# A two-block layer on one core: LRU steps dealt out over a whole period, and GpSimd's products on ScalarE and VectorE

## The chip, the core and the metric

One core of a Trainium2 chip runs the whole program. The metric is the device time of one execution in microseconds; each run of a kernel gives one time. Engines are named as the profile names them: PE is TensorE's matmul, PEld its weight load, DVE VectorE, ACT ScalarE, POOL GpSimd, SP SyncE, which issues most of the transfers.

## What is computed

Two layers follow each other on one sequence of 512 positions and 1024 channels, in float32. The first layer normalises the input, projects it, and merges three branches: a state-space scan (SSD), a gated linear recurrent unit (LRU) and attention to 256 memory rows. The second does the same with forgetting attention, an S5 state-space model and another memory attention. Cut to the parts that matter here:

```python
h = rms_norm(x, norm_g)
proj = h @ w_in                       # z, xbc, dt, lru_gate, lru_x, q, gate_logits
xl = causal_dwconv(lru_x, lru_conv_w, lru_conv_b)          # 4 taps
y_lru = rg_lru(xl, ...) * silu(lru_gate)
merged = g0 * (y_ssd @ w_br_ssd) + g1 * (y_lru @ w_br_lru) + g2 * (y_mem @ w_br_mem)

def rg_lru(x, w_a, b_a, w_x, b_x, lam):                    # 16 blocks of 96 channels
    r = sigmoid(x @ w_a + b_a); i = sigmoid(x @ w_x + b_x)
    log_a = -8 * r * softplus(-lam)
    a = exp(log_a); u = sqrt(-expm1(2 * log_a)) * (i * x)
    return scan(h[t] = a[t] * h[t-1] + u[t])
```

## The kernel before

Everything is kept with channels on the 128 partitions and the 512 positions along the free axis, so a tile is 128x512. A float32 product is made of three fast passes: each operand is split into a high part, rounded to TensorE's short format, and the rest, the low part; high x high, low x high and high x low are summed in PSUM. ScalarE makes the high part of a weight tile (`whi`, L267), VectorE the low part (`wlo`, L280).

The program is a list, `prog`, of jobs and steps. A job is one weight tile of up to 128x1024, in two halves; a half is 12 matmuls of 512 columns for a projection (6 or 9 for others). Before each half, `issue` (L237) puts in the loads two jobs ahead, the high part of the weights four halves ahead and the low part three ahead (`split`, `split_low`), then the steps that are due, then the half's matmuls, and after the second half its evacuation. All engines run their instructions in the order in which this writes them. A step is placed by hand: `lay` (L226) puts named steps in front of numbered halves (`x3@8` is step x3 ahead of half 8), and `after(n, f)` (L190) makes f due n halves later. TensorE has PSUM tiles of three kinds: `gtile` and `xtile`, two buffers each, and `stile`, four. A projection can begin only when the evacuation of the one before the last has read its buffer.

Four places matter here:

- **Input's norm** (`norm_steps`, L529, laid out at L716 among the halves of the memory's key and value projections, `kv_jobs`). Steps x0 to x7 load x, Q0 to Q7 square it and add (ScalarE and GpSimd), T0 and T1 make the reciprocal root (statistics, then rows), g0 to g7 multiply by it on GpSimd (L552), f0 to f7 split the result into high and low parts with the gain (L558 ScalarE, L559 VectorE).
- **Warm matmuls** (`warm`, L708): nine 128x128 products of ones at the start.
- **LRU groups** (L912): the 1536 channels go in four groups s = 0 to 3 of three tiles. A group's gates (`lru_gate`, with the small matmuls for blocks that cross tiles, whose operands `lru_edges` copies between partitions by DMA) take four short halves; then come the three `lru_sg` projections, whose silu is kept, between which `lru_a` (decay `la`, its square on GpSimd, L867, and two products), `lru_b` (square root on ScalarE, then product and scan, L879 and L880) and `lru_c` (product with the silu on GpSimd, L891, and the split of the result, `split_y`) are put in. Then come the projections of the next group (`lru_in`: convolution of four taps, L783 and three times L785, and a split) and the filler: the eight halves that project this group's result, summed into `acc`.
- **Second block's first projections** (L1766): k, v, q and gate of the first pair of heads. `fox_vt` (step v0, L1659) turns v by four transposes (L1663).

Of the kernel before, what the change touches and what calls it, by code (L numbers as in the profile page):

```python
# [171 lines left out]
def two_blocks(ctx, tc, A, out):  # L172
# [356 lines left out]
    def norm_steps(src, gain, dst, queue):  # L529
# [21 lines left out]
        def times(k):  # L551
            return lambda: G.tensor_tensor(st["x"][k], st["x"][k], st["r"], ALU.mult)  # L552

        def fin(k):
            def run():
                x = st["x"][k]
                hi, lo = hp_tile("hhi", k, F32R), hp_tile("hlo", k, F32R)
                S.activation(hi, x, AF.Copy, scale=gain(k))  # L558
                V.scalar_tensor_tensor(lo, x, gain(k), hi.bitcast(F32), ALU.mult, ALU.subtract)  # L559
                dst.append((hi, lo))  # L560
            return run
# [146 lines left out]
    def warm():  # L708

        ps = stile()  # L710
        for _ in range(9):
# [4 lines left out]
    lay(kvj, "c0@1 c1@1 c2@1 c3@1 s4@3 s5@2 s6@2 s7@2 x0@4 x1@4 t0@5 x2@6 t1@7 Q0@7 x3@8 Q1@8 x4@10 Q2@10 x5@12 Q3@12 x6@14 Q4@14 x7@15 Q5@16 "  # L716
        "Q6@18 Q7@19 T0@21 T1@22 g0@22 g1@23 g2@23 g3@23 f0@24 g4@24 f1@25 g5@25 f2@26 g6@26 "
        "f3@27 g7@27 f4@28 f5@29 f6@30 f7@31",
# [60 lines left out]
    add(closed("mlp"), opened("lrp"), g2b[3:])  # L779
# [77 lines left out]
    def lru_a(s):  # L857
        L = lru[s]

        def tile_(j):  # L860
# [6 lines left out]
            G.tensor_tensor(a2, a, a, ALU.mult)  # L867
# [3 lines left out]
        for j in range(3):  # L871
            after(j, (lambda j: lambda: tile_(j))(j))

    def lru_b(s):
        L = lru[s]

        def tile_(j):
# [3 lines left out]
        for j in range(3):  # L881
            S.activation(L["r"][0][j], L["r"][0][j], AF.Sqrt, scale=-1.0 / 16)
        for j in range(3):
            after((j if s == 3 else j + 1) if j < 2 or s < 3 else 2, (lambda j: lambda: tile_(j))(j))

    def lru_c(s):
        L = lru[s]

        def tile_(j):
# [3 lines left out]
        for j in range(3):  # L893
# [18 lines left out]
    for s in range(4):  # L912
        add(lru_gate(s, 0), lru_gate(s, 1))
        add(lru_sg(s, 0), lambda s=s: lru_a(s), lru_sg(s, 1), lambda s=s: lru_b(s), lru_sg(s, 2),
# [1069 lines left out]
```

## Time and profile before

| what | value |
|---|---|
| median of three runs | 1688.86 us (1682.77, 1688.86, 1692.17) |
| the profiled execution | 1688.69 us, its span 1687.0 us |
| PE busy | 1630.0 us, 97% |
| DVE busy | 1160.3 us, 69% |
| ACT busy | 784.7 us, 47% |
| POOL busy | 440.4 us, 26% |

The span is the time from the first to the last instruction that the profiler saw. All times in rows are microseconds from its start. A busy share is an average over all stages, so what a change in one stage is worth has to be read from that stage's own rows: who waits there, for whom, and what follows the wait. Matmuls overlap, so the busy time of PE is that of modelled intervals; how fast TensorE goes is better read from how many matmuls a piece of the chain of waits holds and how long that piece is.

### The profile page before, as it was taken

What the parts mean: (1) busy time and instruction counts of PE and PEld (TensorE: products, weight loads), DVE (VectorE), ACT (ScalarE), POOL (GpSimd) and SP (SyncE); (2) the same over time, 40 slices, a digit from 0 to 9 for tenths busy, and PEclk for the clock granted to TensorE, in tenths of its full rate; (3) what the DMA queues carried; (4) which work ended last, traced back from release to release, by engine and by line L of the source; (5) the groups of instructions that cost most, each with busy time, mean ns of one, the idle gap of its engine ahead of it and who ended that gap; (6) DMA issues with size and microseconds to landing.
All of it is one profiled execution on the core that took longest, in us unless ns stands there. A gap on an engine that the chain in (4) does not pass through costs nothing.

```text
span 1687.0 us, 23007 instructions
## 1 busy us (share of the span) xinstructions
PE 1630.0 (97%) x8202; PEld 1333.5 (79%) x8202; DVE 1160.3 (69%) x1871; ACT 784.7 (47%) x1532; POOL 440.4 (26%) x636
## 2 busy tenths in 40 slices
PE   9999999999999999999999999998999999999998
PEld 8788887787788787878787786777787888888886
DVE  7753267768645987687767886888887545775554
ACT  6554345654543545554544654334344333544334
POOL 4200001211201422213143493665656000020002
PEclk9999999999999999999999999999999999999999
DMA  7322233243323343333432555444334323232532
GB/s 246 120 66 87 85 115 94 90 130 100 95 89 121 106 124 122 97 120 109 133 109 97 177 159 183 109 121 107 102 97 106 122 86 105 94 103 91 174 101 87
DMA packets 112834, 193.01 MB, mean 114 GB/s; under 512 B 50576, under 2 KB 57892, under 8 KB 112720
## 3 DMA queue, kind: packets, MB, share of 16 engines
q1 hardware_dynamic: 97984, 181.41, 34.5%
q10 hardware_dynamic: 14736, 10.14, 2.2%
q8 instruction: 65, 1.06, 0.3%
q14 instruction: 49, 0.40, 0.1%
HBM read 173.90 MB, written 9.54 MB: 109 GB/s over the span
## 4 chain that ended last, share of the span: by engine, by line
PE 67%; DVE 20%; ACT 5%; issue 4%; DMA 3%; POOL 0%; SPq 0%; ACTq 0%; DVEq 0%; POOLq 0%
PE g L351 47%; PE x L351 6%; DVE wlo L280 4%; PE s L351 1%; PE s L1931 1%; DMA rstd<-rs_d 1%; DVE mx L1693 1%; ACT whi L267 1%; DVE P L1700 1%; PE x L1103 1%; PE x L1720 1%; DVE acc L1641 1%; DVE ys L1137 1%; PE x L1107 1%; DVE rg L879 1%
## 5 line engine op out<-in xcount | busy, mean ns | idle before, releaser
L351 PE MATMUL g<-hlo,whi 128*128 128x512 f32 x1304 | 515.9, 396 | 0.0
L280 DVE TENSOR_TENSOR wlo<-wraw,whi 128x512 fp32r<-128x512 f32 (+1 forms) x556 | 424.8, 778 | 102.9 <-ACT whi L267 91.4
L267 ACT ACTIVATE whi<-wraw 128x512 fp32r<-128x512 f32 (+1 forms) x556 | 331.1, 607 | 234.7 <-PE g L351 98.5
L351 PE MATMUL g<-hhi,whi 128*128 128x512 f32 x832 | 331.7, 399 | 10.5 <-DVE xl L785 8.2
L351 PEld LDWEIGHTS g<-hlo,whi 128*128 128x128 f32 x1304 | 249.1, 191 | 51.0 <-issue 1.0
L351 PE MATMUL g<-hhi,wlo 128*128 128x512 f32 x832 | 224.4, 392 | 0.0
L351 PE MATMUL g<-mrg,whi 128*128 128x512 f32 x536 | 219.6, 410 | 0.0
L351 PEld LDWEIGHTS g<-hhi,whi 128*128 128x128 f32 x832 | 157.3, 189 | 47.5 <-issue 11.4
L351 PEld LDWEIGHTS g<-hhi,wlo 128*128 128x128 f32 x832 | 157.6, 189 | 33.6
L351 PE MATMUL g<-mrg,wlo 128*128 128x512 f32 x536 | 144.4, 391 | 0.0
L351 PEld LDWEIGHTS g<-mrg,whi 128*128 128x128 f32 x536 | 103.5, 193 | 22.9 <-issue 1.9
L351 PEld LDWEIGHTS g<-mrg,wlo 128*128 128x128 f32 x536 | 101.6, 190 | 22.2
L351 PE MATMUL g<-y,whi 128*128 128x512 f32 x432 | 114.2, 399 | 5.0 <-DVE t L785 2.3
L867 POOL TENSOR_TENSOR t<-la 128x512 f32<-128x512 f32 x12 | 18.2, 1514 | 321.6 <-ACT la L864 321.6
L351 PEld LDWEIGHTS g<-y,whi 128*128 128x128 f32 x432 | 79.9, 188 | 27.4 <-issue 2.7
L351 PE MATMUL x<-y,whi 128*128 128x512 f32 x336 | 85.3, 393 | 0.5 <-ACT whi L267 0.5
L785 DVE SCALAR_TENSOR_TENSOR t<-g,p,t 128x511 f32<-128x511 f32 (+2 forms) x72 | 53.9, 748 | 38.3 <-ACT t L783 36.6
L1080 POOL TENSOR_SCALAR_AFFINE_SELECT M<-M 128x512 f32<-128x512 f32 x32 | 25.5, 802 | 200.7 <-DMA M<-acs_d 94.7
L351 PEld LDWEIGHTS x<-y,whi 128*128 128x128 f32 x336 | 62.8, 188 | 14.9 <-ACT whi L267 1.3
L1859 POOL TENSOR_TENSOR hhi<-hhi,t 128x512 f32<-128x512 f32 x8 | 13.0, 1626 | 222.1 <-DVE t L1858 210.6
L351 PE MATMUL g<-y,wlo 128*128 128x512 f32 x216 | 61.4, 393 | 0.0
L1694 ACT ACTIVATE P<-P,mx 128x128 f32<-128x128 f32 (+3 forms) x48 | 27.0, 563 | 69.1 <-DVE mx L1693 66.0
(593 smaller groups left out, 2798.7 us busy)
## 6 DMA issues: line engine op xcount, KB each, us to landing
wraw<-in_w_in SPq DMA_DIRECT2D x164, 512.0 KB, 3.3
M<-acs_d SPq DMA_DIRECT2D x32, 256.0 KB, 4.5
wraw<-in_w_ssd SPq DMA_DIRECT2D x16, 512.0 KB, 3.4
wraw<-in_w_out SPq DMA_DIRECT2D x16, 512.0 KB, 3.5
wraw<-in_w_v SPq DMA_DIRECT2D x12, 512.0 KB, 3.7
wraw<-in_w_mem SPq DMA_DIRECT2D x12, 512.0 KB, 3.3
wraw<-in_w_lru SPq DMA_DIRECT2D x16, 384.0 KB, 3.0
wraw<-in_w_k SPq DMA_DIRECT2D x11, 512.0 KB, 4.8
```

The costliest lines, as they stand in the source:

```text
L267: S.activation(hi, raw, AF.Copy)
L280: V.tensor_tensor(lo, raw, hi.bitcast(F32), ALU.subtract)
L351: PE.matmul(ps, w, X[k0 + k][low], start=(k0 + p == 0), stop=(k0 + n == nk and p == 3 * n - 1))
L785: V.scalar_tensor_tensor(dst[:, sft:], ps[:, :512 - sft], c1(cwn, (3 - sft) * nt + j), dst[:, sft:], ALU.mult, ALU.add)
L867: G.tensor_tensor(a2, a, a, ALU.mult)
L879: V.tensor_tensor(u, u, L["r"][0][j], ALU.mult)
L1080: G.affine_select(M, M, [[0, 4], [1, 128]], ALU.is_ge, NEG, base=0, channel_multiplier=-1)
L1103: PE.matmul(py[64 * q_:64 * q_ + 64, c * 128:c * 128 + 128], R["xdt"][:, c, (2 * j + q_) * 64:(2 * j + q_) * 64 + 64], M[:, c])
L1107: PE.matmul(po[:, c * 128:c * 128 + 128], R["prev"][c][:, j * 128:j * 128 + 128], R["C"][:, c * 128:c * 128 + 128])
L1137: V.scalar_tensor_tensor(y, y, c1("ssd_ng", 4 * g + i), R["rs"], ALU.mult, ALU.mult)
L1641: V.tensor_tensor(kl[a][hf], t[hf], k[a][hf].bitcast(F32), ALU.subtract)
L1694: S.activation(P[:, :n], P[:, :n], AF.Exp, bias=mx[:, 0:1], accum_out=mx[:, 1:2])
```

## The change

- In the LRU groups the steps are one function, `lru_steps`, called after the first silu projection; it deals the steps out over the halves that follow: gates at 0, 2 and 4, the three roots at 5, product and scan at 6, 8 and 10, the product with the silu at 12, 14 and 16. The split of the result goes into the next group's gate halves (`lru_parts` at 1, 2 and 3). In the last group, which has no next one, the products come at 8, 9 and 11.
- So a group's result is projected one group later: the filler of group s is the projection of group s - 1. Group 0 has no earlier result; its filler is two gate projections and the second half of the memory branch, which stood ahead of the groups before. Between the first `lru_in` projections and the first gates stand three gate projections, six halves, instead of the memory branch's eight.
- The square of the decay is a Square on ScalarE and the product with the silu a product on VectorE, 12 of each; both were on GpSimd.
- In the input's norm, VectorE multiplies x by gain and reciprocal root in one operation (`scalar_tensor_tensor`), eight times, in place of GpSimd; the split is then a plain one. The steps are laid out anew: loads and squares sooner, statistics three halves sooner, products and splits from half 20 to 31.
- Twelve warm matmuls instead of nine.
- v0 stands ahead of half 7 of the second block's first projections instead of half 5.

```diff
         def times(k):
-            return lambda: G.tensor_tensor(st["x"][k], st["x"][k], st["r"], ALU.mult)
+            return lambda: V.scalar_tensor_tensor(st["x"][k], st["x"][k], gain(k), st["r"], ALU.mult, ALU.mult)
         def fin(k):
             def run():
-                x = st["x"][k]
                 hi, lo = hp_tile("hhi", k, F32R), hp_tile("hlo", k, F32R)
-                S.activation(hi, x, AF.Copy, scale=gain(k))
-                V.scalar_tensor_tensor(lo, x, gain(k), hi.bitcast(F32), ALU.mult, ALU.subtract)
+                split_to(hi, lo, st["x"][k])
...
-        for _ in range(9):
+        for _ in range(12):
...
-    lay(kvj, "c0@1 c1@1 c2@1 c3@1 s4@3 s5@2 s6@2 s7@2 x0@4 x1@4 t0@5 x2@6 t1@7 Q0@7 x3@8 Q1@8 x4@10 Q2@10 x5@12 Q3@12 x6@14 Q4@14 x7@15 Q5@16 "
...
+    lay(kvj, "c0@1 c1@1 c2@1 c3@1 s4@3 s5@2 s6@2 s7@2 x0@4 x1@4 t0@5 x2@6 t1@7 x3@7 Q0@7 x4@8 Q1@8 Q2@9 x5@10 Q3@10 x6@11 x7@12 Q4@12 "
...
-    add(closed("mlp"), opened("lrp"), g2b[3:])
+    add(closed("mlp"), opened("lrp"))
...
-            G.tensor_tensor(a2, a, a, ALU.mult)
+            S.activation(a2, a, AF.Square)
...
+        def times(j):
             u = L["r"][1][j]
-            G.tensor_tensor(u, u, L["sg"][j], ALU.mult)
-            L["Y"].append(split_y(u))
-        for j in range(3):
-            after(0 if s == 3 else j + 1, (lambda j: lambda: tile_(j))(j))
+            V.tensor_tensor(u, u, L["sg"][j], ALU.mult)
+
+        staged(gates, 0, 2, 4)
+        staged(roots, 5)
+        staged(scan, 6, 8, 10)
+        staged(times, *((8, 9, 11) if s == 3 else (12, 14, 16)))
+        if s == 3:
+            staged(lambda j: lru_parts(3, j), 11)
+
+    def lru_parts(s, j):
+        lru[s]["Y"].append(split_y(lru[s]["r"][1][j]))
 
     add([lru_in(0, j) for j in range(3)])
-    add(branch_jobs(A["w_mem"], 4, Late(Ym, 4), 4, mem_last, xtile))
+    add(g2b[3:6])
...
     for s in range(4):
...
+        if s:
+            add((lambda s: lambda: staged(lambda j: lru_parts(s - 1, j), 1, 2, 3))(s))
+        add(lru_gate(s, 0), lru_gate(s, 1), lru_sg(s, 0), lambda s=s: lru_steps(s), lru_sg(s, 1), lru_sg(s, 2))
         if s < 3:
-            br = branch_jobs(A["w_lru"], 4 * s, Late(lru[s]["Y"], 0), 3, acc_first() if s == 0 else acc_add, xtile)
-            add([lru_in(s + 1, j) for j in range(3)], br)
+            add([lru_in(s + 1, j) for j in range(3)])
+        add(fill if s else [g2b[6:], branch_jobs(A["w_mem"], 4, Late(Ym, 4), 4, mem_last, xtile)])
+        fill = branch_jobs(A["w_lru"], 4 * s, Late(lru[s]["Y"], 0), 3, acc_first() if s == 0 else acc_add, xtile)
+    add(lambda: [lru_parts(3, j) for j in (1, 2)])
...
-    lay(fi, "u0@2 n0@5 v0@5 n1@6",
+    lay(fi, "u0@2 n0@5 n1@6 v0@7",
```

`staged(f, *at)` makes f(j) due at[j] halves later. What the change moves on VectorE is seen at three places. The first is group 2, from the last silu projection to the first tile of the next group. L455 ends a silu, L879 and L880 are product and scan of one tile, L388 is the low half of a result, L785 the convolution. VectorE's order before:

```order
L455 SCALAR_TENSOR_TENSOR sg<-t,g 128x512
L280 TENSOR_TENSOR wlo<-wraw,whi 128x512
L879 TENSOR_TENSOR rg_3333<-rg_3333,rg_3299 128x512
L880 SCALAR_TENSOR_TENSOR rg_3333<-la,rg_3333 128x512
L388 TENSOR_TENSOR y<-rg_3313,y 128x512
L280 TENSOR_TENSOR wlo<-wraw,whi 128x512
L388 TENSOR_TENSOR y<-rg_3325,y 128x512
L785 SCALAR_TENSOR_TENSOR xl<-g,p_92,xl 128x511
```

And now, where the same lines are L455, L880, L881, L388 and L783, with L870 and L871 for the two products of a gate:

```order
L870 SCALAR_TENSOR_TENSOR rg_3208<-rg_3208,xl 128x512
L871 SCALAR_TENSOR_TENSOR rg_3170<-t,rg_3170 128x512
L455 SCALAR_TENSOR_TENSOR sg<-t,g 128x512
L280 TENSOR_TENSOR wlo<-wraw,whi 128x512 x2
L880 TENSOR_TENSOR rg_3188<-rg_3188,rg_3146 128x512
L881 SCALAR_TENSOR_TENSOR rg_3188<-la,rg_3188 128x512
L783 SCALAR_TENSOR_TENSOR xl<-g,p_92,xl 128x511
```

Ahead of the convolution of the first next tile stands one scan, that of tile 0, and no low half of a result; the other two scans have moved behind it.

The second place is the end of group 3. Before, VectorE's last steps stood with the last silu (L455) ahead of the split of the next small job's weights (L276):

```order
L879 TENSOR_TENSOR rg_3834<-rg_3834,rg_3800 128x512
L880 SCALAR_TENSOR_TENSOR rg_3834<-la,rg_3834 128x512
L455 SCALAR_TENSOR_TENSOR sg<-t,g 128x512
L388 TENSOR_TENSOR y<-rg_3814,y 128x512
L388 TENSOR_TENSOR y<-rg_3826,y 128x512
L388 TENSOR_TENSOR y<-rg_3834,y 128x512
L276 TENSOR_TENSOR whi<-wraw,whi 128x4x32
```

Now the sums of the filler (L675) stand among the products with the silu (L885) and the scans:

```order
L880 TENSOR_TENSOR rg_3701<-rg_3701,rg_3663 128x512
L881 SCALAR_TENSOR_TENSOR rg_3701<-la,rg_3701 128x512
L885 TENSOR_TENSOR rg_3689<-rg_3689,sg 128x512
L675 TENSOR_TENSOR acc<-acc,x 128x512
L280 TENSOR_TENSOR wlo<-wraw,whi 128x384
L885 TENSOR_TENSOR rg_3701<-rg_3701,sg 128x512
```

The last silu has gone ahead of all of these, and each sum has a step of the group before or behind it.

The third place is the input's norm, VectorE again. Before, from the end of the first value projection (VVl), a split of x (L559) stood between two low halves of weights, and its product was GpSimd's:

```order
L393 TENSOR_TENSOR KTl<-t,KT 128x256
L601 SCALAR_TENSOR_TENSOR VVl<-g,mrc,VV 128x512 x2
L559 SCALAR_TENSOR_TENSOR hlo<-acc,p_92,hhi 128x512
L280 TENSOR_TENSOR wlo<-wraw,whi 128x512
```

Now each of its steps is a split (L393) and a product (L552), and they begin ahead of the end of that projection:

```order
L393 TENSOR_TENSOR hlo<-acc,hhi 128x512
L552 SCALAR_TENSOR_TENSOR acc<-acc,p_92,rstd 128x512
L280 TENSOR_TENSOR wlo<-wraw,whi 128x512
L393 TENSOR_TENSOR KTl<-t,KT 128x256
L599 SCALAR_TENSOR_TENSOR VVl<-g,mrc,VV 128x512 x2
```

VectorE has two operations per tile of x where it had one, and three tiles have been begun when that projection ends.

## Rows read from the trace of the kernel before

**Rows 1.** The page: busy time, share of the span, instructions of each engine.

```profile
PE 1630.0 (97%) x8202; PEld 1333.5 (79%) x8202; DVE 1160.3 (69%) x1871; ACT 784.7 (47%) x1532; POOL 440.4 (26%) x636
```

**Rows 2.** Waits of PE: who waited for whom, us in total, times, longest.

```profile
PE g L351 <- DVE xl L785: 8.2, 3, 2.7
PE x L597 <- DVE wlo L280: 3.1, 3, 1.7
...
PE s L1663 <- DVE t L1325: 2.8, 1, 2.8
...
PE g L938 <- DVE sg L455: 2.2, 1, 2.2
...
PE g L351 <- ACT whi L267: 1.1, 1, 1.1
```

**Rows 3.** The chain that ended last: start us, length us, what, number.

```profile
244.31 5.50 PE g L351 x24
...
274.40 7.32 PE g L351 x24
...
451.93 5.53 PE g L938 x16
...
1035.49 9.79 PE g L351 x36
```

**Rows 4.** Stretches: length, busy us of each engine (instructions), granted clock, DMA share, GB/s.

```profile
10.00:15.00 5.00, 5.00 (x25) 4.98 (x24) 4.23 (x9) 3.42 (x8) 1.80 (x3) 0.50 0.60 224
274.40:277.80 3.40, 3.40 (x9) 2.63 (x10) 3.37 (x6) 1.66 (x3) 0.00 (x0) 0.53 0.37 116
```

**Rows 5.** DVE in time, group 0: start, length, line, operation, names, shapes, number.

```profile
253.91 1.53 DVE L868 SCALAR_TENSOR_TENSOR rg<-rg,xl 128x512 f32<-128x512 f32 x1
...
259.21 0.68 DVE L280 TENSOR_TENSOR wlo<-wraw,whi 128x512 fp32r<-128x512 f32 x1
259.82 0.68 DVE L879 TENSOR_TENSOR rg<-rg,rg 128x512 f32<-128x512 f32 x1
260.53 1.23 DVE L880 TENSOR_TENSOR_SCAN rg<-la,rg 128x512 f32<-128x512 f32 x1
...
262.25 1.79 DVE L879 TENSOR_TENSOR rg<-rg,rg 128x512 f32<-128x512 f32 x1
...
271.95 2.30 DVE L785 SCALAR_TENSOR_TENSOR xl<-g,p,xl 128x511 f32<-128x511 f32 x3
```

**Rows 6.** POOL in time, group 0.

```profile
253.36 1.53 POOL L867 TENSOR_TENSOR t<-la 128x512 f32<-128x512 f32 x1 [0.70 <-ACT la L864]
...
261.90 1.59 POOL L891 TENSOR_TENSOR rg<-rg,sg 128x512 f32<-128x512 f32 x1 [4.96 <-DVE rg L880]
```

**Rows 7.** ACT by line, 0 to 70 us: busy us, mean ns, idle before.

```profile
L424 ACT ACTIVATE t<-acc 128x512 f32<-128x512 f32 x8 | 5.0, 620 | 0.3 <-DMA acc<-in_xT 0.3
```

**Rows 8.** ACT in time, group 0: the load of the square root's table.

```profile
256.65 1.28 ACT L882 ACT_TABLE_LOAD   x1
```

**Rows 9.** The copies into the edge tiles xe, from issue to landing.

```profile
DMA to landing us min/median/max: 2.6/3.9/5.5
```

**Rows 10.** DVE in time, the input's norm.

```profile
50.99 1.73 DVE L559 SCALAR_TENSOR_TENSOR hlo<-acc,p,hhi 128x512 fp32r<-128x512 f32 x1
...
57.70 1.79 DVE L559 SCALAR_TENSOR_TENSOR hlo<-acc,p,hhi 128x512 fp32r<-128x512 f32 x1
```

**Rows 11.** POOL in time, the input's norm.

```profile
46.45 12.49 POOL L552 TENSOR_TENSOR acc<-acc,rstd 128x512 f32<-128x512 f32 x8 [5.07 <-ACT rstd L419]
```

**Rows 12.** DVE in time, second block's first projections.

```profile
1034.13 0.65 DVE L1325 SCALAR_TENSOR_TENSOR t<-g,r 128x512 f32<-128x512 f32 x1
...
1039.88 0.69 DVE L1323 TENSOR_TENSOR t<-g,r 128x512 f32<-128x512 f32 x1 [3.05 <-PE g L351]
```

**Rows 13.** POOL in time, the same place.

```profile
1040.30 1.68 POOL L1674 TENSOR_SCALAR_AFFINE_SELECT nbm<-nb 128x512 f32<-128x512 f32 x2 [15.93 <-DMA nb<-n_d]
```

**Rows 14.** PE in time, the first scores.

```profile
1045.13 0.28 PE L1686 MATMUL s<-hhi 128*128 128x256 f32 x1
```

More of the change, by code (lines that the diff above doesn't have):

```diff
@@ L715, in two_blocks @@
     named = {"c": msc[4:], "t": mstat, "Q": xsq, "s": msq, "T": xstat, "f": xfin, "g": xrow, "x": xload}
-    lay(kvj, "c0@1 c1@1 c2@1 c3@1 s4@3 s5@2 s6@2 s7@2 x0@4 x1@4 t0@5 x2@6 t1@7 Q0@7 x3@8 Q1@8 x4@10 Q2@10 x5@12 Q3@12 x6@14 Q4@14 x7@15 Q5@16 "
-        "Q6@18 Q7@19 T0@21 T1@22 g0@22 g1@23 g2@23 g3@23 f0@24 g4@24 f1@25 g5@25 f2@26 g6@26 "
-        "f3@27 g7@27 f4@28 f5@29 f6@30 f7@31",
+    lay(kvj, "c0@1 c1@1 c2@1 c3@1 s4@3 s5@2 s6@2 s7@2 x0@4 x1@4 t0@5 x2@6 t1@7 x3@7 Q0@7 x4@8 Q1@8 Q2@9 x5@10 Q3@10 x6@11 x7@12 Q4@12 "
+        "Q5@13 Q6@15 Q7@16 T0@18 T1@19 g0@20 f0@21 g1@21 f1@23 g2@23 f2@24 g3@24 f3@26 g4@26 f4@27 g5@27 f5@29 g6@29 f6@30 g7@30 "
+        "f7@31",
         {k + str(i): f for k, v in named.items() for i, f in enumerate(v)})
@@ L853, in lru_gate, with staged, lru_steps, gates @@
         return Job(A["lru_w"][2 * s + gate], [384, 384], [first, second])
-    def lru_a(s):
+    def staged(f, *at):
+        for j, n in enumerate(at):
+            after(n, (lambda j: lambda: f(j))(j))
+    def lru_steps(s):
         L = lru[s]
-        def tile_(j):
+        def gates(j):
             tr, ti = L["r"][0][j], L["r"][1][j]
@@ L870, in tile_, with roots, scan @@
             L["a"][j] = a
-        for j in range(3):
[L872 to L877, printed above, removed]
+        def roots(_):
+            for j in range(3):
+                S.activation(L["r"][0][j], L["r"][0][j], AF.Sqrt, scale=-1.0 / 16)
+        def scan(j):
             u = L["r"][1][j]
@@ L880, in tile_ @@
             V.tensor_tensor_scan(u, L["a"][j], u, 0.0, ALU.mult, ALU.add)
[L881 to L889, printed above, removed]
-            u = L["r"][1][j]
-            G.tensor_tensor(u, u, L["sg"][j], ALU.mult)
-            L["Y"].append(split_y(u))
-        for j in range(3):
-            after(0 if s == 3 else j + 1, (lambda j: lambda: tile_(j))(j))
+        def times(j):
+            u = L["r"][1][j]
+            V.tensor_tensor(u, u, L["sg"][j], ALU.mult)
[7 more added lines that the diff above has]
+        lru[s]["Y"].append(split_y(lru[s]["r"][1][j]))
     add([lru_in(0, j) for j in range(3)])
-    add(branch_jobs(A["w_mem"], 4, Late(Ym, 4), 4, mem_last, xtile))
+    add(g2b[3:6])
     th1 = {}
@@ L912, in two_blocks @@
     for s in range(4):
-        add(lru_gate(s, 0), lru_gate(s, 1))
-        add(lru_sg(s, 0), lambda s=s: lru_a(s), lru_sg(s, 1), lambda s=s: lru_b(s), lru_sg(s, 2),
-            lambda s=s: lru_c(s))
+        if s:
+            add((lambda s: lambda: staged(lambda j: lru_parts(s - 1, j), 1, 2, 3))(s))
+        add(lru_gate(s, 0), lru_gate(s, 1), lru_sg(s, 0), lambda s=s: lru_steps(s), lru_sg(s, 1), lru_sg(s, 2))
         if s < 3:
-            br = branch_jobs(A["w_lru"], 4 * s, Late(lru[s]["Y"], 0), 3, acc_first() if s == 0 else acc_add, xtile)
-            add([lru_in(s + 1, j) for j in range(3)], br)
+            add([lru_in(s + 1, j) for j in range(3)])
+        add(fill if s else [g2b[6:], branch_jobs(A["w_mem"], 4, Late(Ym, 4), 4, mem_last, xtile)])
+        fill = branch_jobs(A["w_lru"], 4 * s, Late(lru[s]["Y"], 0), 3, acc_first() if s == 0 else acc_add, xtile)
+    add(lambda: [lru_parts(3, j) for j in (1, 2)])
     add(closed("lrp"), opened("ssp"))
```

## Prediction

> **What bounds the kernel now.** The page says that TensorE is busy 97% of the span [rows 1], but that is not the whole story: its matmul ends are modelled. I read three things. First, who TensorE waits for [rows 2]: nearly every wait of over 1 us names VectorE, so the span is TensorE's own work plus a short list of places where VectorE came late. Second, what a wait costs beyond itself [rows 3, 4]: 24 matmuls of one projection take 5.50 us undisturbed (0.229 us each) and 7.32 us right after the 2.73 us wait, with the clock granted at 0.53 over those 3.4 us, that is, mostly at the lower of its two levels. Third, why VectorE was late [rows 5, 6]. The change touches four such places: the LRU groups, the input's norm, the first matmuls, and one transpose of the second block. The waits in the second block's attention windows it does not touch.
>
> **LRU groups: what goes.** There is one such wait in each of the four groups: three on L785, 8.2 us, and one on L455, 2.2 us [rows 2]; 10.4 us together. After each the clock is low: three times 24 matmuls in 7.3 instead of 5.50 us, 1.8 each, and 16 in 5.53 us against 16 x 0.229 = 3.67, 1.9 [rows 3]; 7.3 us together. So 17.7 us are at stake.
>
> Why VectorE is late: at 253.9 to 271.9 it runs without a gap. The three-step convolution L785 of the next group's first tile, which frees one of the two PSUM buffers, stands behind scans, products and halves of Y. Operations that take 0.68 us alone take 1.53 and 1.79 us beside a product of GpSimd, and both end some 0.55 us after that product does [rows 5, 6]. The change does two things about it. GpSimd gets nothing any more in this stage: its twelve squares become ScalarE's (a Square of 128x512 takes 0.62 us [rows 7]), its twelve products VectorE's (0.61 us from one start to the next, as at 259.21 [rows 5]). And the steps are dealt out over up to sixteen halves of jobs instead of some six, with the halves of Y in the next group.
>
> Here the Trainium skill has a rule, in "SBUF — State Buffer", the section on the single rule of the shared port: a VectorE operation with two SBUF inputs and a GpSimd operation that reads SBUF block each other until one is finished. The two rows just named agree with it. By that rule the whole excess goes with GpSimd; if something else made those operations long, the third rival below applies.
>
> **LRU groups: what comes instead.** Take the stretch in which VectorE now has most to do: in group 2, from the end of the first next projection to the end of the eight filler halves with their sums into acc. TensorE needs 4 x 2.75 + 8 x 9 x 0.229 = 27.5 us. VectorE has three convolutions (2.30 each), two pairs of product and scan (0.71 + 1.23), fourteen sums, products and halves (0.61), one weight half of 512 columns (0.61) and twelve of 384 (0.48, an estimate from the 0.61) [rows 5]: 6.9 + 3.9 + 8.5 + 0.6 + 5.8 = 25.7 us. It fits, with 1.8 us to spare. Followed through in order, the convolution of the first tile is done 3.0 us after its projection, 2.4 us before its PSUM buffer is wanted; that of the third some 14.4 us after, and the sum of the first filler half behind it at 15.5, while the third filler half wants that buffer at 15.1; the next sum is 0.3 us late too. So some 0.7 us of waits return in group 2. Group 3 has no projections but puts scans, products and sums into the same eight halves (16.5 us of work on 16.5): another 0.5. In group 1 ScalarE copies the sums; it has three of them per 6.2 us beside weight halves of 0.5, and does not fill up. In group 0 the last memory projections have moved into the group: 1.8 us of VectorE per half of 2.75.
>
> ScalarE gets 3 x 0.62 for the squares in the stage of the gates' products, and a table load (1.28 us [rows 8]) now ahead of the next group's first gate instead of the second silu. Six gate tiles cost 3.6 there, weights 2.1, halves of Y 1.9, in all 8.9 us on 6.9 us of matmuls. The lag of 2 us is covered by the four PSUM buffers, as the fifth tile wants the first's buffer 4.6 us in and has it at 2.5. SyncE keeps its order but for one place: in group 0 the edge copies have six filler halves of 2.75 us behind the projections instead of eight. They are issued one behind the other from the fourth half on and land 2.6 to 5.5 us after issue [rows 9]; the gates now come 3 x 2.75 = 8.3 us after that half's start instead of 13.8. I take 0, at most 1 us lost.
>
> Sum: 17.7 - 1.2 = 16.5 us gained; bounds 8 (half the waits return) and 17.7.
>
> **Input's norm.** TensorE waits 3.1 us for wlo in the last value projection [rows 2]. From 50.99 to 59.49 VectorE takes 8.5 us for five operations, 1.7 each, while GpSimd has its eight products, 12.5 us from 46.45 on [rows 10, 11]; alone they take some 0.7 [rows 5]. Now VectorE has eight more operations, 8 x 0.65 = 5.2 us, and loses 5 x 1.0 = 5 us of excess there and some before; the work begins three halves of 6 x 0.229 us earlier, 4 us. The squares' sums stay on GpSimd but are packed closer, over nine halves instead of twelve, so their excess falls into a stretch where VectorE is already full: up to 1 us back. The x loads come sooner in SyncE's queue, ahead of some loads of weights: the same eight loads in nine halves instead of twelve, 0 to 1 us. I take 2.7 gained; bounds 4 gained and 1 lost.
>
> **Three more warm matmuls.** From 10 to 15 us the clock is at 0.50 [rows 4] and 25 matmuls, of 256 columns, start in 5 us: 0.20 each, against 0.115 by half of the 0.229 for 512. Between the nine warm ones and the first real one TensorE waits 1.1 us for whi [rows 2]; three more fill about that. If the clock then stays high, the 25 could take 2.1 us less, but the halves that follow are soon bound by the arrival of weights and by VectorE; I take two thirds of it, 1.4, as the most, 0.2 lost if the clock falls anyway and the warm ones end late, and 0.8 as the value.
>
> **Transpose of v, second block.** L1663 waits 2.81 us for v, which on VectorE stands behind the softplus and its scan and starts at 1034.13 [rows 2, 12]. Then 36 matmuls take 9.79 us against 36 x 0.229 = 8.25: 1.5 us of low clock [rows 3]. Two halves later nothing waits for v but the gate projection, which wants v's PSUM buffer: v is read by 1034.8, and the half ahead of it, 2.75 us long and begun where the wait began, ends at about that time: 0.2 returns. The window behind starts earlier and needs the forget sums: the two masks are made from them from 1040.3 on, 1.68 us for both, while the first scores, at 1045.13 before, would come at 1041 [rows 13, 14]: it just fits. 4.1 gained; bounds 1 and 4.3.
>
> **The sum.** 16.5 + 2.7 + 0.8 + 4.1 = 24.1 us. The profiled execution took 1688.7 us, with a span of 1687.0; the median of the three runs is 1688.9 (they spread from 1682.8 to 1692.2). 1688.7 - 24.1 = 1664.6; I forecast **1664**.
>
> **Rivals.**
> 1. VectorE stays late in the LRU groups. For: in the projections of the next group, 5.2 to 5.65 us of VectorE now stand against 5.5 of TensorE for each pair of halves, and the scans still come ahead of the convolutions. If the order slips by over 2.4 us, the wait for the PSUM buffer returns, and with it the low clock. Against: the followed order above. Half of the waits: 8 to 9 us less, 1673. Chance 0.13.
> 2. The 4.1 us of v go to a later wait: the window's softmax may hang on transfers and not on TensorE, and L1708 then waits that much longer. 1668. For: the masks come only at 1040.9. Against: VectorE sits idle 3.05 us until 1039.88, waiting for TensorE [rows 12]. Chance 0.14.
> 3. Slower: VectorE's operations stay long without GpSimd. Place: the stretch from the next projections to the last filler half. VectorE's work there, counted as above, is about 33, 20, 25 and 16.5 us in groups 0 to 3, and TensorE's 44, 27.5, 27.5 and 16.5. At 1.5 times the length the excess is 6 + 3 + 10 + 8 = 27 us, which eats the gain; at twice it is 22 + 13 + 23 + 17 = 75, and the kernel ends at some 1740. It decides from 1.5 on. For: lengths of twice and more are in [rows 5, 10]. Against: all of them lie beside a GpSimd operation, which is now gone. Chance 0.03.
> 4. The change does not do what it says, because the late steps land where VectorE waits for ScalarE's chain and block the halves of weights behind them: then only the other three places gain, 7.6 us: 1681. Chance 0.05.
>
> **How the numbers follow.** The forecast has 0.65, the rivals 0.13, 0.14, 0.03 and 0.05. The range for 8 in 10 takes in the forecast's bounds, the spread of the runs (some 4 us to either side) and rivals 1 and 2: 1655 to 1675. Half a percent is 8.4 us, about what a measurement of this kernel can tell from no change. All but rivals 3 and 4 lie below 1680.4, and rival 4 lies next to that line, on either side: faster 0.94, same 0.03, slower 0.03.
>
> **What would show it.** Right: L785, L938 and L1663 (under their new line numbers) gone from what TensorE waits for, no stretch of low clock at the four places of the LRU groups nor before the first window, and VectorE's operations in the LRU groups all near 0.68 us. In the last value projection there should be under 1 us of waits for wlo, and the granted clock at 10 to 15 us should be above 0.50. A wait for acc sums of some 0.5 us should appear in groups 2 and 3. Wrong: long VectorE operations without GpSimd, new waits at the gates for ScalarE or the edges, or a longer wait at L1708 in the first window.

## Result, and the profile after

The changed kernel takes 1666.05 us (median of four executions, 1665.58 to 1667.17) against 1686.68 (1682.77 to 1692.17) for the one before: a ratio of 0.9876, with a 95% interval of 0.9845 to 0.9907. The forecast was 1664 and faster; so the sign, the size and the range held. The gain is 20.6 us by these medians, where the sum of the prediction had 24.1. One of the reasons given for it did not hold, as the experiments show.

The page of the changed kernel, which answers to [rows 1]:

```profile
PE 1621.1 (97%) x8208; PEld 1330.2 (80%) x8208; DVE 1143.9 (69%) x1891; ACT 789.5 (47%) x1544; POOL 388.8 (23%) x604
```

Whom TensorE waits for now (us in total, times, longest), to be read beside [rows 2]. The convolution of the LRU groups, their last silu, v and wlo have gone from the list; three short waits of the start have come in, for whi, for the memory's squares (L510) and behind ScalarE's squares of x (L424); the wait for whi right behind the warm matmuls has gone. The L783 line is a convolution of a later stage that was there before.

```profile
PE s L1711 <- DVE mx L1702: 18.5, 6, 4.5
PE g L351 <- DVE t L783: 2.0, 4, 0.9
...
PE s L351 <- ACT whi L267: 1.5, 1, 1.5
...
PE x L398 <- POOL t L510: 1.1, 1, 1.1
...
PE s L351 <- ACT t L424: 0.8, 1, 0.8
```

The chain that ended last, in the LRU stage (start, length, what, number), beside [rows 3]. 128 matmuls follow each other at 0.227 us each and 96 at 0.229, where three pieces of 24 took 7.3 us; the small projection behind the groups (L938 before, L941 now) takes 3.67 us for its 16 instead of 5.53.

```profile
224.78 29.01 PE g L351 x128
253.79 21.99 PE x L351 x96
...
435.29 3.67 PE g L941 x16
```

The stretch from the first q projection to the end of that small projection, which holds the same work in both kernels (length, busy us of each engine with its instructions, granted clock, DMA share, GB/s), in the changed kernel and then in the one before:

```profile
62.30:438.80 376.50, 375.28 (x1705) 308.92 (x1704) 231.04 (x391) 203.64 (x362) 0.00 (x0) 1.00 0.33 101
```

```profile
63.50:457.30 393.80, 382.94 (x1706) 312.58 (x1704) 241.52 (x378) 197.84 (x349) 36.59 (x24) 0.98 0.31 95
```

VectorE has thirteen more operations there (the twelve products and one at the edge) and is busy 10.5 us less, and the granted clock is 1.00 throughout. By stages, from the starts of the same matmuls in both traces: start to first q projection 1.2 us less; q projections and LRU groups, with the 1.9 us of low clock behind L938, 17.4 less; state-space branch to the forget gates' job 1.9 less; second block's first projections 4.2 less; windows 0 to 5 2.2 more; the rest 0.6 less. That makes 23.1, the difference of the spans (1687.0 and 1663.9); it is more than the 20.6 of the medians, because the profiled execution of the kernel before (1688.69) was longer than its median.

### The profile page after: what moved, and what is told of

Read it like the earlier page. It is cut to its first block, busy times and chain, and to the rows that moved or that the text cites. A ratio compares the mean times of both kernels' runs of the same rounds, so it can differ in the third digit from the quotient of the medians.

```text
span 1663.9 us, 23009 instructions
## 1 busy us (share of the span) xinstructions
PE 1621.1 (97%) x8208; PEld 1330.2 (80%) x8208; DVE 1143.9 (69%) x1891; ACT 789.5 (47%) x1544; POOL 388.8 (23%) x604
## 4 chain that ended last, share of the span: by engine, by line
PE 73%; DVE 17%; DMA 4%; ACT 3%; issue 2%; POOL 0%; SPq 0%; DVEq 0%; ACTq 0%; POOLq 0%
PE g L351 52%; PE x L351 6%; DVE wlo L280 3%; PE s L1934 1%; DMA rstd<-rs_d 1%; DVE mx L1696 1%; DVE P L1703 1%; PE x L1106 1%; PE x L1723 1%; DVE acc L1644 1%; DVE ys L1140 1%; PE x L1110 1%; PE s L344 1%; PE s L351 1%; PE s L342 1%
## 5 line engine op out<-in xcount | busy, mean ns | idle before, releaser
L280 DVE TENSOR_TENSOR wlo<-wraw,whi 128x512 fp32r<-128x512 f32 (+1 forms) x556 | 409.2, 753 | 84.6 <-ACT whi L267 72.3
L351 PEld LDWEIGHTS g<-y,whi 128*128 128x128 f32 x432 | 79.8, 188 | 27.6 <-issue 2.5
L783 DVE SCALAR_TENSOR_TENSOR t<-g,p,t 128x511 f32<-128x511 f32 (+2 forms) x72 | 53.9, 748 | 38.3 <-ACT t L781 36.6
L1326 DVE TENSOR_TENSOR t<-g,r 128x512 f32<-128x512 f32 (+1 forms) x41 | 28.2, 689 | 35.0 <-PE g L351 35.0
```

The lines of the kernel that those rows point to most:

```text
L280: V.tensor_tensor(lo, raw, hi.bitcast(F32), ALU.subtract)
L351: PE.matmul(ps, w, X[k0 + k][low], start=(k0 + p == 0), stop=(k0 + n == nk and p == 3 * n - 1))
L783: V.scalar_tensor_tensor(dst[:, sft:], ps[:, :512 - sft], c1(cwn, (3 - sft) * nt + j), dst[:, sft:], ALU.mult, ALU.add)
L1326: V.tensor_tensor(dst, ps, r2, ALU.mult)
```

## Experiments

Each kernel differs from the changed kernel (or, where said, from the one before) by the diff shown. Ratios are to the kernel before, executed beside it. Its medians were 1686.4, 1687.4 and 1688.1 us in the three sets of runs, so medians from different sets can be compared to within a us or two. Stages within the traces are steadier: from the first q projection to the start of the small projection behind the groups it is 388.4 us in the kernel before and 372.8 to 372.9 us in all nine kernels, the changed one among them, that have the new order and the later projection with nothing added.

| kernel | median us | ratio to before, 95% interval |
|---|---|---|
| lru_alone | 1672.19 | 0.9921 (0.9903 to 0.9940) |
| engines_only | 1693.60 | 1.0048 (1.0033 to 1.0063) |
| dealt_on_gpsimd | 1665.12 | 0.9878 (0.9863 to 0.9894) |
| v_at_5 | 1670.85 | 0.9911 (0.9897 to 0.9926) |
| norm_as_before | 1668.25 | 0.9886 (0.9871 to 0.9900) |
| warm_nine | 1665.98 | 0.9875 (0.9858 to 0.9891) |
| later_convolution | 1674.8 | one execution |
| bunched_steps | 1674.41 | 0.9918 (0.9902 to 0.9935) |
| late_transposes | 1653.55 | 0.9797 (0.9783 to 0.9812) |
| transposes_at_9 | 1653.19 | 0.9789 (0.9773 to 0.9806) |
| together | 1653.70 | 0.9797 (0.9782 to 0.9812) |

**The LRU part alone.** In the changed kernel the norm, the warm matmuls and v0 are put back (the lines of the norm, which undo those of the change, are left out here):

```diff
...
-        for _ in range(12):
+        for _ in range(9):
...
-    lay(fi, "u0@2 n0@5 n1@6 v0@7",
+    lay(fi, "u0@2 n0@5 v0@5 n1@6",
```

> The kernel before with the LRU part of the change alone (steps dealt out, squares on ScalarE, products on VectorE, projection one group later); norm, warm matmuls and v0 as before. Theory A (the four LRU places give what the two traces show between the first q projection and the end of the low clock behind the groups, 17.4 us, and the rest of the change the remainder): 17 to 18 us below the kernel before, near 1669, and PE waits 2.7 to 3.1 us for wlo and 2.8 us for v as before. Theory B (part of the gain hangs on the earlier norm): under 14 us. No stretch of low clock between 240 and 460 us under A.

The stage of the q projections and LRU groups is 15.5 us shorter than before and the 1.9 us behind it are gone too: 17.4, as in the changed kernel. The whole gains 14.2 us by the medians and 15.8 by the spans (1687.0 and 1671.2), less than the 17 to 18 that theory A had for it. TensorE, which waited 2.8 us for v before, waits longer here:

```profile
PE s L1668 <- DVE t L1330: 4.0, 1, 4.0
PE x L597 <- DVE wlo L280: 3.2, 3, 1.7
```

So the LRU part stands by itself (theory A on its place). The stage with v, the second block's first projections, is 1.9 us longer than before (33.7 and 31.8), which explains why less of it reaches the end of the trace; the 1.6 us between spans and medians come mostly from the long profiled execution of the kernel before.

**Only the engines moved.** The kernel before, steps in their old places:

```diff
-            G.tensor_tensor(a2, a, a, ALU.mult)
+            S.activation(a2, a, AF.Square)
...
-            G.tensor_tensor(u, u, L["sg"][j], ALU.mult)
+            V.tensor_tensor(u, u, L["sg"][j], ALU.mult)
```

> The kernel before, its LRU steps in their old places, with only the 12 squares on ScalarE and the 12 products on VectorE. Theory P (GpSimd made VectorE late): in group 0 of the kernel before five VectorE operations between 253.3 and 272 us are 0.85, 0.85, 1.11, 0.81 and 1.10 us longer than 0.68, in all 4.7; three products of 0.61 come in, 1.8; VectorE would be 2.9 us earlier at the convolution, and the wait was 2.7, so all three waits at the convolution shrink to under 0.5 us, the low clock there goes, and the kernel ends 13 to 17 us below the one before. Theory D (the bunched order made VectorE late): the three waits stay at 1.5 us or more, low clock behind them, and at most 8 us are gained.

It became slower, by 7.2 us in the medians and 4.9 in the spans, and theory P fell. What TensorE waits for between 224 and 470 us:

```profile
PE g L351 <- DVE xl L785: 9.1, 3, 3.0
PE g L938 <- ACT whi L267: 4.2, 1, 4.2
```

VectorE in time, the same place of group 0 as [rows 5]: every operation that took 1.5 to 1.8 us is at 0.68 to 0.69, and yet the convolution starts at 272.31 instead of 271.95.

```profile
253.92 0.68 DVE L868 SCALAR_TENSOR_TENSOR rg<-rg,xl 128x512 f32<-128x512 f32 x1
255.30 0.69 DVE L869 SCALAR_TENSOR_TENSOR rg<-t,rg 128x512 f32<-128x512 f32 x1 [0.70 <-ACT t L867]
...
267.68 0.67 DVE L891 TENSOR_TENSOR rg<-rg,sg 128x512 f32<-128x512 f32 x1
269.05 0.69 DVE L388 TENSOR_TENSOR y<-rg,y 128x512 fp32r<-128x512 f32 x1 [0.70 <-ACT y L387]
...
272.31 2.32 DVE L785 SCALAR_TENSOR_TENSOR xl<-g,p,xl 128x511 f32<-128x511 f32 x3
```

The numbers in brackets show where the 4.7 us of lengthening went: VectorE now stands still for ScalarE's square and for the high half of the result, some 0.7 us at a time and 3.4 us in all from the first row to the convolution, two of the products (1.2 us) stand ahead of the convolution, and ScalarE's three squares push the roots back by 1.7 us. The roots in the kernel before, then here:

```profile
257.94 1.68 ACT L882 ACTIVATE rg<-rg 128x512 f32<-128x512 f32 x3
```

```profile
259.66 1.68 ACT L882 ACTIVATE rg<-rg 128x512 f32<-128x512 f32 x3
...
451.93 0.63 ACT L387 ACTIVATE y<-rg 128x512 fp32r<-128x512 f32 x1 [4.33 <-DVE rg L891]
```

GpSimd had been slow for its neighbour, but it worked beside the other two; in the bunched order its share came into their chain. At the end of group 3 the same chain holds back the weights: ScalarE waits 4.33 us for the first of three products (the last row) and 1.36 for each of the others before it comes to whi, and TensorE waits 4.2 us for that. Of the 4.9 us between the spans, 2.9 lie in the stage from the first q projection to the end of the small projection (396.7 and 393.8 us) and 1.5 behind the second block's first scores, where the code is the same.

**The dealt-out order with GpSimd.** The opposite edit in the changed kernel: order and later projection as changed, both operations on GpSimd again.

```diff
-            S.activation(a2, a, AF.Square)
+            G.tensor_tensor(a2, a, a, ALU.mult)
...
-            V.tensor_tensor(u, u, L["sg"][j], ALU.mult)
+            G.tensor_tensor(u, u, L["sg"][j], ALU.mult)
```

> The changed kernel with its dealt-out order, but squares and products on GpSimd again. Theory P: VectorE loses 4.7 us per group to GpSimd and is spared 1.8; the slack at the first convolution was 2.4 us, so waits of 0.5 to 2 us return in some groups with low clock behind them: 4 to 12 us above the changed kernel. Theory D: the dealt-out order has room for it, and the kernel stays within 2 us of the changed one (1666).

It is as fast as the changed kernel, as theory D has it. Waits in the LRU stage, and the row of the stretch from the first q projection to the end of the small projection:

```profile
PE x L351 <- DVE acc L675: 0.8, 2, 0.5
PE x L351 <- ACT whi L267: 0.7, 1, 0.7
```

```profile
61.00:437.60 376.60, 375.08 (x1706) 309.00 (x1705) 229.33 (x379) 197.79 (x350) 32.83 (x24) 1.00 0.32 101
```

With the operations of the kernel before (one more at the edge) VectorE is busy 12.2 us less than in it (241.52 to 229.33). The changed kernel without its twelve products more would have 231.04 - 12 x 0.61 = 223.7. So of 17.8 us of lengthening 5.6 remain, and the larger part has gone by the order alone. What remains lies in the low halves of the weights, not in the steps of the groups. The product ahead of the scan, in the kernel before and here, and the low halves of the weights, here and in the changed kernel (busy us, mean ns):

```profile
L879 DVE TENSOR_TENSOR rg<-rg,rg 128x512 f32<-128x512 f32 x12 | 12.6, 1048 | 0.0
```

```profile
L880 DVE TENSOR_TENSOR rg<-rg,rg 128x512 f32<-128x512 f32 x12 | 8.2, 685 | 1.7 <-ACT rg L876 1.7
L280 DVE TENSOR_TENSOR wlo<-wraw,whi 128x512 fp32r<-128x512 f32 (+1 forms) x141 | 94.2, 688 | 41.6 <-ACT whi L267 34.4 <-PE g L351 4.0 <-PE s L836 3.2
```

```profile
L280 DVE TENSOR_TENSOR wlo<-wraw,whi 128x512 fp32r<-128x512 f32 (+1 forms) x141 | 88.5, 647 | 39.1 <-ACT whi L267 32.2 <-PE g L351 3.6 <-PE s L836 3.2
```

So the run shows that the new order does not need the move of the engines. What a lengthened step of the chain would cost in that order it does not show, since GpSimd's work hardly meets those steps any more. One meeting that does not lengthen, GpSimd's product and VectorE's three convolution steps, which take 2.31 us as they do alone:

```profile
242.93 1.66 POOL L885 TENSOR_TENSOR rg<-rg,sg 128x512 f32<-128x512 f32 x1 [4.21 <-DVE rg L881]
```

```profile
243.35 2.31 DVE L783 SCALAR_TENSOR_TENSOR xl<-g,p,xl 128x511 f32<-128x511 f32 x3
```

**How much room the convolution has.** Superfluous products on VectorE, 0.72 us each, are put ahead of the first convolution of the next group, 4, 8 and 12 of them in groups 0, 1 and 2:

```diff
         def ev(ps):
+            if s and not j:
+                for _ in range(4 * s):
+                    x = lru[s - 1]["sg"][2]
+                    V.tensor_tensor(pt("lrp", "more"), x, x, ALU.mult)
             a = pt("lrp", "xl", bufs=5)
```

> The changed kernel with superfluous products on VectorE (0.61 us each) ahead of the first convolution of the next group: 4 in group 0, 8 in group 1, 12 in group 2; 1.21 us of them fall into VectorE's idle time ahead of that convolution. If VectorE's lateness at the convolution is what the LRU groups paid for (theory D), the slack read from the changed kernel, 2.7 to 2.8 us from the end of the convolution to the start of the third projection, decides: delays of 1.2, 3.7 and 6.1 us give waits of 0, about 0.9 and about 3.3 us at the third projection in groups 0, 1 and 2, with low clock behind the last at least; in all 5 to 8 us above the changed kernel. If the gain is due to something else (the later projection alone), none of the three places waits by over 0.3 us.

```profile
PE g L351 <- DVE xl L783: 7.4, 2, 5.2
```

In group 2 the products and the convolution behind them, and the 24 matmuls that follow the wait:

```profile
363.41 8.66 DVE L794 TENSOR_TENSOR more<-sg 128x512 f32<-128x512 f32 x12
371.98 2.31 DVE L783 SCALAR_TENSOR_TENSOR xl<-g,p,xl 128x511 f32<-128x511 f32 x3
```

```profile
374.44 8.23 PE g L351 x24
```

From the end of the scan to the start of the convolution it is 1.2 us in the changed kernel and 2.7, 5.6 and 8.5 here: delays of 1.5, 4.4 and 7.3 us, of which 0, 2.2 and 5.2 (7.4 in two) come out as waits. So VectorE may come some 2.1 to 2.2 us later than it does, and no more. My 2.7 to 2.8 had left out what lies between the end of the convolution and the restart of TensorE, and the products took 0.72 instead of 0.61. The stage is 11.4 us longer: 7.4 of waits, 2.7 of low clock in the 24 matmuls shown (8.23 instead of 5.50 us), the rest in smaller pieces. 8.75 us of it reach the end by the time of this one execution, 9.2 by the span, where 5 to 8 were forecast.

**Bunched steps.** The changed kernel with its engines and its later projection, but the scans and products as one block:

```diff
-        staged(scan, 6, 8, 10)
-        staged(times, *((8, 9, 11) if s == 3 else (12, 14, 16)))
+        staged(scan, *((6, 8, 10) if s == 3 else (6, 6, 6)))
+        staged(times, *((8, 9, 11) if s == 3 else (6, 6, 6)))
```

> The changed kernel with its engines and its later projection, but in groups 0 to 2 all three pairs of product and scan and the three products with the silu due at once, 6 halves on, as a block ahead of the first convolution of the next group. The block holds 2 x 1.94 + 3 x 0.61 = 5.7 us more ahead of that convolution, of which 1.2 us fall into VectorE's idle time; the slack was about 2.2 us (the waits of 2.2 and 5.2 us for superfluous products that delayed the convolution by 4.4 and 7.3). Theory D (the dealing out itself is the gain): a wait of about 2.3 us for the convolution in each of the three groups with low clock behind it, 8 to 13 us above the changed kernel. Rival (the projection one group later is the gain): no waits of over 0.5 us there, within 2 us of the changed kernel.

```profile
PE g L351 <- DVE xl L783: 6.1, 3, 2.1
```

Three waits of 2.0 us in the mean were forecast as 2.3, and the time is 8.4 us above the changed kernel, as theory D says. The stage is 8.0 us longer than in the changed kernel, so dealing out scans and products is worth about half of the LRU gain of 17.4. The last group, which this run leaves as changed, holds another 4.1 (the wait of 2.2 us and 1.9 of low clock before). The remaining 5 us or so come with the rest, above all the later projection, by which the halves of the result leave the block; no run has the dealt-out order without it, so this share is not shown by itself.

**v ahead of half 5 again.**

```diff
-    lay(fi, "u0@2 n0@5 n1@6 v0@7",
+    lay(fi, "u0@2 n0@5 v0@5 n1@6",
```

> The changed kernel with v0 ahead of half 5 again. Theory A (the windows behind took 1.7 us back because they start earlier): the wait for v of 2.8 us and its low clock return, 4.2 us, windows 0 and 1 are 1.7 us shorter, together 2 to 3 us above the changed kernel, 1668 to 1669. Theory B (the windows' longer time has nothing to do with v0): 4 to 4.5 us above it, 1670.

The time is that of theory B, or a little above. The wait, then the stretch behind it:

```profile
PE s L1666 <- DVE t L1328: 4.0, 1, 4.0
```

```profile
1015.40:1018.80 3.40, 3.19 (x10) 2.71 (x11) 2.04 (x4) 0.00 (x0) 0.00 (x0) 0.50 0.50 149
```

The medians differ by 4.8 us, the stage by 6.2 (33.8 to 27.6), since here the wait is 4.0 us where it was 2.8 before. ScalarE waits 5.6 us for a transfer of weights a little earlier, 4.2 in the kernel before. In the four kernels with v at half 5 the two go together: 4.2, 4.7, 5.4 and 5.6 us there, 2.8, 3.2, 4.0 and 4.0 at v.

Windows 0 and 1 take 47.5 and 48.1 us here, 1.7 less than in the changed kernel (48.7 and 48.7), as theory A has it. But this has nothing to do with v: in dealt_on_gpsimd and warm_nine, with v at half 7 too, they take 47.4 and 48.1, and 47.0 and 47.7 us (47.8 and 47.9 in the kernel before). In window 0 of dealt_on_gpsimd the wait at L1711 is the same 2.7 us as in the changed kernel; only the low clock behind it is shorter.

**The norm as before.** Its products on GpSimd, its split and its layout as in the kernel before, twelve warm matmuls kept (the lines of split and layout are left out here):

```diff
-            return lambda: V.scalar_tensor_tensor(st["x"][k], st["x"][k], gain(k), st["r"], ALU.mult, ALU.mult)
+            return lambda: G.tensor_tensor(st["x"][k], st["x"][k], st["r"], ALU.mult)
...
```

> The changed kernel with the input's norm as before (products on GpSimd, the old places of its steps); twelve warm matmuls and everything else as changed. Theory A (the norm gained 3.1 us of waits for wlo and gave about 2 back as waits for whi in the key projections): the waits for wlo of 3.1 us return, the waits for whi and t of 1.5 and 0.8 us go, and the kernel ends 0.5 to 1.8 us above the changed one, 1666.5 to 1668. Theory B (the norm gained the 2.7 us that the prediction took): 2.5 to 3.5 us above it.

```profile
PE x L597 <- DVE wlo L280: 3.1, 3, 1.7
```

The kernel is 2.2 us above the changed one by the medians, which come from different sets of runs. The waits for whi and behind the squares have gone, and one of 0.8 us behind VectorE (L573) stands in their place. The stage from the memory's column sums to the first q projection takes 45.7 us, 2.0 more than in the changed kernel (43.7). In seven other kernels with the changed norm it takes 43.1 to 43.4, and in the three others with the old norm 45.0. So the norm gains between 1.4 and 2.6 us, less than the 2.7 forecast; the 2.2 us of the medians lie between the two theories.

**Nine warm matmuls.**

```diff
-        for _ in range(12):
+        for _ in range(9):
```

> The changed kernel with nine warm matmuls instead of twelve. Theory A (the shorter low clock at the start was given back at the column sums of the memory, which wait for GpSimd's squares): the low clock there lasts 6.8 us again instead of 3.4, the wait of 1.1 us for the squares goes, and the time is that of the changed kernel within 0.8 us. Theory B (the warm matmuls gain what the prediction took): 0.8 to 1.4 us above it.

There is no difference (1665.98 and 1666.05), but not by A's mechanism: with nine, the clock is at 1.00 here from 8 to 20 us. The rows for 10 to 15 us of warm_nine and of the changed kernel, beside [rows 4]:

```profile
10.00:15.00 5.00, 5.00 (x32) 4.93 (x32) 4.01 (x8) 4.02 (x10) 2.08 (x2) 1.00 0.61 219
```

```profile
10.00:15.00 5.00, 5.00 (x34) 4.98 (x33) 3.59 (x8) 3.37 (x8) 1.17 (x2) 0.74 0.63 242
```

Three kernels have the very same code up to there, with nine: the clock over these 5 us is 0.50 in the kernel before, 0.53 in engines_only and 1.00 in lru_alone. So the number of warm matmuls does not settle the clock there; what does was not tried.

**A version that beats both.** The waits in the second block's windows, which the change leaves alone, are the largest that remain. In window 1 of the changed kernel the normalised P comes late to the last transposes; ahead of it on VectorE stands L1644, two operations in 3.23 us beside GpSimd's work, where two took 1.4 us at 1008.97:

```profile
1097.00 3.23 DVE L1644 TENSOR_TENSOR acc<-t,hhi 64x512 fp32r<-64x512 f32 x2
```

```profile
1097.95 1.73 POOL L1482 TENSOR_TENSOR NBi<-NBi,x 128x512 f32<-128x512 f32 x1
```

The last transposes of windows 0 to 4 are moved by one half:

```diff
-              "t02@3 t03@4 s12@4 s13@4 n10@4 n11@4 nb@5 t10@6 t11@6 n12@6 n13@6 y@5 M1@6 t12@7 t13@7 vt@8 wc@8 u@8 "
+              "t02@3 t03@4 s12@4 s13@4 n10@4 n11@4 nb@5 t10@6 t11@6 n12@6 n13@6 y@5 M1@6 t12@8 t13@8 vt@8 wc@8 u@8 "
```

> The changed kernel with one step of the second block's windows 0 to 4 moved: the last transposes of P (t12, t13) stand ahead of half 8 instead of half 7. In the changed kernel TensorE waits 18.5 us there for VectorE, 3 to 4.5 us a window. Theory A (VectorE's place in time does not depend on TensorE's there): a half of 2.75 us covers as much of each wait, 10 to 14 us less and most of the low clock behind the waits gone, 3 to 10 us more: 1642 to 1653. Theory B (VectorE waits there for transfers that start later in turn): under 5 us less.

```profile
PE s L1711 <- DVE mx L1702: 8.7, 6, 1.8
```

9.8 us of waits go with the half (18.5 to 8.7), and the granted clock over the span rises from 0.991 to 0.997: 12.5 us less than the changed kernel, and 2% less than the one before. That is theory A, half a us above its times (1642 to 1653) and just short of its 10 to 14 us of waits.

Two halves later, with the product with v moved behind the last half:

```diff
-              "t02@3 t03@4 s12@4 s13@4 n10@4 n11@4 nb@5 t10@6 t11@6 n12@6 n13@6 y@5 M1@6 t12@7 t13@7 vt@8 wc@8 u@8 "
-              "pv@9")
+              "t02@3 t03@4 s12@4 s13@4 n10@4 n11@4 nb@5 t10@6 t11@6 n12@6 n13@6 y@5 M1@6 t12@9 t13@9 vt@8 wc@8 u@8 "
+              "pv@10")
```

> The changed kernel with the last transposes of P (t12, t13) of windows 0 to 4 ahead of half 9 and the product with v (pv) behind the last half, so two halves later than in the changed kernel. With one half later five waits of 1.8 to 1.9 us remained. If VectorE's place in time does not depend on TensorE's, they go entirely: 9 us less than with one half later, some 1644 to 1647 with the low clock behind them. Rival: the product with v, now directly ahead of the next window's scores, waits for ScalarE's copies of the transposes or delays the scores: within 3 us of 1653.5, or above.

```profile
PE s L1666 <- DVE t L1328: 4.4, 4, 1.2
PE s L1711 <- DVE wlo L280: 2.6, 3, 0.9
PE x L1595 <- DVE Hb L1586: 2.3, 4, 0.6
PE s L1711 <- DVE mx L1702: 2.2, 5, 0.5
```

The second half of delay gains nothing. The wait at L1711 falls to 2.2 us, and TensorE now waits for VectorE elsewhere: at v's transposes, for the low half of weights and for Hb. The time is the rival's, but its places hold little of it (1.0 us of waits at the scores, 1.2 at a transpose that waits for ScalarE's copy). From the first scores to the last VectorE is busy 91% of the time here, 82% in the changed kernel.

The last run is this one with the loads and squares of x spread a little more:

```diff
-    lay(kvj, "c0@1 c1@1 c2@1 c3@1 s4@3 s5@2 s6@2 s7@2 x0@4 x1@4 t0@5 x2@6 t1@7 x3@7 Q0@7 x4@8 Q1@8 Q2@9 x5@10 Q3@10 x6@11 x7@12 Q4@12 "
+    lay(kvj, "c0@1 c1@1 c2@1 c3@1 s4@3 s5@2 s6@2 s7@2 x0@4 x1@4 t0@5 x2@6 t1@7 x3@8 Q0@8 Q1@9 x4@9 Q2@10 x5@11 Q3@12 x6@12 Q4@13 x7@13 "
```

> The kernel with the transposes ahead of half 9, and the input's norm with its first loads of x and squares spread over one to two halves more (statistics and products in the changed kernel's places). If the waits of 1.5 and 0.8 us in the key projections come from squares on ScalarE that wait for x ahead of the halves of weights, they shrink to under 1 us together and the stage up to the first q projection is 1 to 1.5 us shorter: 1 to 1.5 us below the kernel with the transposes ahead of half 9. Otherwise it is the same within 0.5 us.

The stage takes 43.0 instead of 43.1 us: two waits behind VectorE (L571), 1.7 us together, have gone from the key projections, and two behind ScalarE's squares, 1.5 us together, stand in their place. This was a miss: in every kernel with the changed norm the key projections wait some 1.5 to 2.3 us, now for one engine and now for the other.

## Why the prediction was right, and where it was not

- **The sum, 24.1 us.** The traces show 23.1, the medians 20.6. By stages 1.2 us came instead of 3.5 up to the first q projection (norm and warm matmuls), 17.4 instead of 16.5 in the LRU groups, 4.2 instead of 4.1 at v, and 0.3 on balance outside the terms. The forecast started from 1688.7 us, 2 us above the median that the kernel before turned out to have. That 1664 lies within 2.1 us of the measured median is thus in part luck: the terms missed on both sides.
- **LRU, 16.5 us.** 17.4 came, near the upper bound, and the rows asked for are there: no wait for the convolution or the silu, clock 1.00 from 62.3 to 438.8. The slack of 2.4 us followed by hand measured 2.1 to 2.2. The forecast waits of 1.2 us in groups 2 and 3 were 0.7 us for whi in group 2 and 0.5 us for acc sums (two) in group 3; the sizes were right and one engine was off.
- **The reason given first, GpSimd.** The step "why VectorE is late" named two causes: the order, and operations of 1.5 to 1.8 us beside a product of GpSimd. The rows were read rightly (they shrink to 0.68 in engines_only). The Trainium skill's rule ("SBUF — State Buffer", "Who interferes with whom", the single rule) agrees with that, and, as a rule on two inputs in SBUF, with the convolution of 2.31 us above, which has one of its inputs in PSUM. The conclusion, that the move to ScalarE and VectorE helps, was the step that failed: taking GpSimd out gains nothing in the new order (1665.12 with it, 1666.05 without) and loses 0.5% in the old one. The rule of the Trainium skill is one on single operations; what counted here is the chain between three engines. The sum did not show the error, because it took the waits that disappear from the waits themselves and never split them by cause.
- **Norm, 2.7 us.** 1.4 to 2.6 in the runs. wlo's 3.1 us went, and VectorE's split and product take 0.68 and 0.74 us there instead of 1.7, as forecast. The term that was too small is "squares packed closer" and "x loads sooner", at most 1 us each: in the changed kernel TensorE waits 1.5 us for whi and 0.8 us behind ScalarE's squares in the key projections.
- **Warm matmuls, 0.8 us.** Nothing came. The clock was 0.74 instead of 0.50 and TensorE started 34 instead of 25 matmuls in those 5 us, as asked for; but TensorE then waited 1.1 us for the memory's squares on GpSimd, and warm_nine and lru_alone have the clock at 1.00 with the old number. The step took one execution's clock for a property of the kernel.
- **v, 4.1 us.** 4.2 in the two traces and 4.8 in the medians of v_at_5. Nothing late took its place: the first scores come at 1020.39, and the second of the rivals, a longer wait in the first window, did not happen: the longest wait there is 2.7 us in the changed kernel, 2.8 in v_at_5 and 3.8 in the kernel before.
- **Rivals.** The first needed a slip of more than 2.4 us; later_convolution and bunched_steps show that the slack was about what it said, and what passing it costs (8.4 us for three waits of 2). The third did not happen: VectorE's operations are short without GpSimd. The mechanism of the fourth, late steps that hold ScalarE ahead of the weights, is real, but in engines_only (4.2 us for whi), not in the changed kernel.
- **What balanced.** Outside the terms the windows gave 2.2 us back and the state-space branch gained 1.9; both move by that much between kernels with the same code there (window 0 takes from 47.0 to 49.0 us, the state-space branch from 554.0 to 556.4), so no effect of the change can be read from them.

## What to carry to other kernels

An operation that two engines make long for each other is not yet a cost: ask whether the engine that took the work over stands in the chain, and test the new order with the old engines before crediting the move. Late evacuations cost nothing as long as they are within the slack of the PSUM buffers, here 2.1 us; each us beyond it came out as a wait, and behind the longest the low clock took another 2.7 us. A wait that remains can be moved off by placing the waiting step one half later, but only as far as the engine behind it has room: the first half of 2.75 us here gave 12.5 us over five windows, the second nothing more.

## What the runs showed of the hardware

- The granted clock at the start differed between kernels with the same warm-up: over 10 to 15 us it was 0.66 to 1.00 in the nine kernels with twelve matmuls and 0.50 to 1.00 in the four with nine.
- After equal waits the time at the lower level differed: in window 0, after the wait of 2.7 us for L1702 and a second of 0.9 us, the clock is at 0.50 over 6.8 us in the changed kernel.

```profile
1053.70:1060.50 6.80, 6.00 (x16) 4.79 (x17) 3.64 (x3) 3.61 (x8) 6.44 (x7) 0.50 0.46 121
```

The same stretch of dealt_on_gpsimd, which has the same two waits there and whose window 0 is 1.2 us shorter:

```profile
1053.70:1060.50 6.80, 5.91 (x24) 4.89 (x24) 4.37 (x5) 3.70 (x9) 6.73 (x7) 0.75 0.45 120
```

- VectorE's convolution step, which takes one operand from PSUM, kept its 2.31 us for three beside a GpSimd product of 1.66 us, while products of two SBUF tiles took 1.5 to 1.8 us beside one [rows 5, 6].
